# A 16-expert layer behind two transformer blocks on one core: where the modulation's matrix product runs

## The chip, the core and the metric

One Trainium2 chip, one of its cores. The metric is device time in microseconds, the median of the runs; lower is better. The engines are TensorE (matmuls, PE in the profile; PEld is its weight load), VectorE (DVE), ScalarE (ACT), GpSimd (POOL) and SyncE (SP), which here only issues transfers.

## The reference, cut to what matters

256 tokens of width 1024 pass through a first block (FFN, a token mixer with three attentions, FFN) and a second one (a mixer with a long convolution and a recurrence, then 16 experts of which each takes 32 tokens). Everything is float32. The second block is modulated by a vector c, and a context by c_ctx:

```python
def modulation(cvec, p):
    return jnp.split(jax.nn.silu(cvec) @ p['mod_w'] + p['mod_b'], 6, axis=-1)

m_lat = modulation(c[:, None, :], p)      # mod_w: 1024 x 6144
m_ctx = modulation(c_ctx, p)
h = rmsnorm(x, p['norm1_pre']) * (1.0 + m_lat[1]) + m_lat[0]
mixed, _ = token_mixer_2(h, p, ctx_states)
x = x + m_lat[2] * rmsnorm(mixed, p['norm1_post'])
h2 = rmsnorm(x, p['norm2_pre']) * (1.0 + m_lat[4]) + m_lat[3]
x = x + m_lat[5] * rmsnorm(expert_choice_moe(h2, p), p['norm2_post'])
```

So one or two rows are multiplied with a matrix of 1024 x 6144, 25 MB. The context needs parts 0 and 1 alone.

## The kernel before, in words

The stages follow each other: first FFN (to about 310 us), attention mixer (to about 640), second FFN (to about 880), second mixer (to about 1180), experts (to the end).

`ffn` (L365) walks over the hidden width in 11 groups of 256 columns. For each group four weight tiles of 128 x 1024 are loaded by SP (`wraw`, four buffers, rows of 1 KB), ScalarE copies each to a rounded high part `wh`, VectorE subtracts it for the low part `wl` (`wsplit`, L261; two buffers each), and TensorE makes three products per tile pair, hh with wh, hl with wh and hh with wl (`proj_feat_acc`, L292, its matmuls at L299, L301, L302): 96 matmuls a group. ScalarE and VectorE then form the gated product (L390 to L392), and at the end of group i `hooks.get(i)` is called: it traces other work there. Hook -1 is called before the first group. Behind the groups `wide` (L335) makes the down projection.

`modulation` (L797) is a generator. It treats mod_w in three blocks of 2048 columns: block 0 holds parts 0 and 1, block 1 parts 2 and 3, block 2 parts 4 and 5. It makes `sc`, 128 x 8 x 32, of which columns 0 and 1 are silu(c) and silu(c_ctx) and the rest zero. Per block the matrix comes in 16 pieces of 128 x 1024 (`mraw`, three buffers, 512 KB, rows of 4 KB), issued from GpSimd's queue at L835.

- Block 0 is traced in the first FFN's hook -1 (`start`, L1882). Each piece holds two column quarters of 512; TensorE multiplies each with `sc` into a column group of its own (32 columns of the array, 32 partitions of the PSUM tile `px`), L839. A matmul of float32 is two records in the trace.
- Blocks 1 and 2 are traced in the second FFN (`filter_and_modulation`, L1896, and hooks 6 and 10). Each piece is scaled by ScalarE (L842, L846) and added to `acc` by GpSimd (L847), or scaled and added by VectorE (L844, for k = 4). When all pieces are in, TensorE sums over the partitions with a column of ones, four quarters, L852.

At the end of a block the bias `m` is added, for blocks 1 and 2 the norm gains `nr` are worked in, and the rows go to DRAM (`mrows`, L867); the loads of `m` (L824) and `nr` (L861) and the stores are issued from ScalarE's queue. `psX`, the PSUM pool of `px`, has two banks; in the second FFN the convolution's filter (`hyena_filter`, L1304) uses it too: its sine layers ahead of the modulation, its second half behind it.

The order of each engine's instructions is set by a planner: it goes through its own estimate of the times and gives an engine, of the instructions that are ready by that estimate, the one that was traced first. On the chip each engine then takes its instructions in that order. Where work is traced, and so where a generator yields, is its rank.

Of the kernel before, what the change touches and what calls it, by code (L numbers as in the profile page):

```python
# [11 lines left out]
F32 = mybir.dt.float32  # L12
F32R = mybir.dt.float32r
I32 = mybir.dt.int32
ALU = mybir.AluOpType
AF = mybir.ActivationFunctionType
# [4 lines left out]
KC = 8  # L21
DFF = 2816
# [12 lines left out]
POOL_SHARE = 256  # L35
HOOK0 = 3
HOOK1 = 4
HOOK2 = 6
HOOK3 = 10
LGS = 4  # L40
GATHERS = {0: 1, 1: 1, 2: 2, 4: 2, 6: 2}
RINGS = (1, 2, 1, 2, 2, 4, 1, 3, 1, 1, 1)
# [123 lines left out]
def _body(nc, tc, ctx, A, out):  # L166
    V, S, G, PE = nc.vector, nc.scalar, nc.gpsimd, nc.tensor
# [10 lines left out]
    psX = ctx.enter_context(tc.tile_pool(name="psX", bufs=2, space=PSUM))  # L178
# [7 lines left out]
    xt = []  # L186
# [12 lines left out]
    def P(name, i=0, n=1):  # L199
        a = PP_COLS[name][0]  # L200
        return pp[:, a + i:a + i + n]
# [116 lines left out]
    def new_hT():  # L318
        return (hpool.tile([128, KC, T], F32R, name="hh"), hpool.tile([128, KC, T], F32R, name="hl"))
# [477 lines left out]
    def modulation(side, blocks, after=None):  # L797

        with ExitStack() as fx:
            tmp = fx.enter_context(tc.tile_pool(name="md_t", bufs=1, side=side))
            cr = tmp.tile([16, 128], F32, name="cr")
            S.dma_start(cr, A["c2"])
            th = tmp.tile([16, 128], F32, name="cth")
            S.activation(th, cr, AF.Tanh, scale=0.5)
            V.tensor_scalar(th, th, 0.5, 0.5, op0=ALU.mult, op1=ALU.add)
            V.tensor_tensor(cr, cr, th, op=ALU.mult)
            pt = psT.tile([128, 4, 128], F32, name="tr")  # L810
            PE.transpose(pt[:, 0, :16], cr, ident[:16, :16])
            sc = tmp.tile([128, KC, 32], F32, name="sc")
            V.memset(sc, 0.0)
            V.tensor_copy(sc[:, :, 0], pt[:, 0, 0:8])
            V.tensor_copy(sc[:, :, 1], pt[:, 0, 8:16])
            one = tmp.tile([128, 32], F32, name="one")
            V.memset(one, 0.0)
            V.memset(one[:, 0:1], 1.0)
            mbv = A["mod_b_2"].rearrange("(b g n) -> b g n", b=3, g=4)
            for b in blocks:  # L820
                m = tmp.tile([128, 512], F32, name="m")
                V.memset(m, 0.0)
                for g in range(4):
                    S.dma_start(m[32 * g:32 * g + 2, :], mbv[b, g:g + 1, :].to_broadcast([2, 512]))  # L824
                if b:
                    acc = tmp.tile([128, 2048], F32, name="acc")
                else:
                    ps = psX.tile([128, 512], F32, name="px")
                for k in range(KC):
                    for hf in range(2):  # L830
                        raw = tmp.tile([128, 1024], F32, name="mraw", bufs=3)
                        if after is not None and 2 * k + hf < 3:
                            G.tensor_copy(raw[:, 0:1], after)
                        hs = slice(hf * 1024, hf * 1024 + 1024)
                        G.dma_start(raw, A["mod_w_2"][k * 128:(k + 1) * 128, b * 2048 + hf * 1024:b * 2048 + hf * 1024 + 1024])  # L835
                        if b == 0:
                            for gg in range(2):
                                g = hf * 2 + gg
                                PE.matmul(ps[32 * g:32 * g + 32, :], sc[:, k, :], raw[:, gg * 512:gg * 512 + 512],  # L839
                                          start=(k == 0), stop=(k == KC - 1), skip_group_check=True)  # L840
                        elif k == 0:
                            S.activation(acc[:, hs], raw, AF.Copy, scale=sc[:, k, 0:1])  # L842
                        elif k % 4 == 0:
                            V.scalar_tensor_tensor(acc[:, hs], raw, sc[:, k, 0:1], acc[:, hs], op0=ALU.mult, op1=ALU.add)  # L844
                        else:
                            S.activation(raw, raw, AF.Copy, scale=sc[:, k, 0:1])  # L846
                            G.tensor_tensor(acc[:, hs], acc[:, hs], raw, op=ALU.add)  # L847
                if b:
                    yield
                    ps = psX.tile([128, 512], F32, name="px")  # L850
                    for g in range(4):
                        PE.matmul(ps[32 * g:32 * g + 32, :], one, acc[:, g * 512:g * 512 + 512], start=True, stop=True,  # L852
                                  skip_group_check=True)
                V.tensor_tensor(m, ps, m, op=ALU.add)
                if b:
                    nr = tmp.tile([128, 512], F32, name="nr")
                    V.memset(nr, 1.0)
                    for v in range(2):
                        nm = (None, ("norm1_post_2", None), ("norm2_pre_2", "norm2_post_2"))[b][v]
                        for g in range(2 * v, 2 * v + 2 if nm else 0):  # L860
                            S.dma_start(nr[32 * g:32 * g + 1, :], A[nm].rearrange("(h n) -> h n", h=2)[g % 2:g % 2 + 1, :])  # L861
                    lo, hi = m[0:64], m[64:128]
                    V.scalar_tensor_tensor(lo, lo, 0.5 if b == 1 else 1.0, nr[0:64], op0=ALU.mult if b == 1 else ALU.add,
                                           op1=ALU.mult)
                    V.tensor_tensor(hi, hi, nr[64:128], op=ALU.mult)
                for g in range(4):
                    S.dma_start(mrows[b * 4 + g:b * 4 + g + 1, :], m[32 * g:32 * g + 1, :])  # L867
                if b:
                    continue
                pt = psT.tile([128, 4, 128], F32, name="tr")  # L870
                for q in range(4):
                    PE.transpose(pt[:, q, :], m[:, q * 128:(q + 1) * 128], ident)
                mT = tmp.tile([128, 4, 4, 2], F32, name="mT")
                V.tensor_copy(mT, pt.rearrange("p q (g r) -> p q g r", g=4)[:, :, :, 0:2])

                n1 = P("n1pre", 0, 8).rearrange("p (g q) -> p g q", q=4)
                for r in range(2):
                    mv = mT.rearrange("p q g r -> p r g q")[:, r]
                    V.scalar_tensor_tensor(mfm[:, r, 0, :].rearrange("p (g q) -> p g q", q=4), mv[:, 2:4, :], 1.0,
                                           n1, op0=ALU.add, op1=ALU.mult)  # L880
                    V.tensor_copy(mfm[:, r, 1, :].rearrange("p (g q) -> p g q", q=4), mv[:, 0:2, :])
# [5 lines left out]
    def norm_mod_T(hT, t, x, r, xn, us, dense=True):  # L887

        rs = rsqrt(mean_sq_halves(x, xn), 128, 1, 1e-6)
        last = V.tensor_scalar(xn, x, rs, None, op0=ALU.mult)  # L890
        sl = slice(t * 128, (t + 1) * 128)

        def put(j0, k, ps):
            u = us(j0)
            for j in range(k):
                c = j0 + j
                if j0 and dense:
                    S.activation(u[:, j, :], ps[:, j, :], AF.Identity, scale=mfm[:, r, 0, c:c + 1],
                                 bias=mfm[:, r, 1, c:c + 1])
                else:  # L900
                    V.tensor_scalar(u[:, j, :], ps[:, j, :], mfm[:, r, 0, c:c + 1], mfm[:, r, 1, c:c + 1],
                                    op0=ALU.mult, op1=ALU.add)
            split(hT[0][:, j0:j0 + k, sl], hT[1][:, j0:j0 + k, sl], u)
        return last, lambda: transposes(put, xn, KC, dense)
# [975 lines left out]
    mods = []  # L1880
# [8 lines left out]
    hT2 = attention(xt, hT1, A["ffn2_norm"])  # L1889
# [15 lines left out]

    hT3 = []

    def norm_mod(pool, scratch):
        hT3.extend(new_hT())
        us = [scratch[:, 2 * D + i * 512:2 * D + i * 512 + 512].rearrange("p (a b) -> p a b", a=4) for i in range(4)]  # L1910

        normed = []

        def after(t):
            normed.append(norm_mod_T(hT3, t, xt[t], 0, scratch[:, t * D:(t + 1) * D], lambda j0: us[t * 2 + j0 // 4]))
            if t:
                in_turn(normed)
                next(filt[0], None)
        return after

    ffn(xt, hT2, None, A["ffn2_w_gate"], A["ffn2_w_up"], A["ffn2_w_down"], {-1: filter_and_modulation, HOOK2: lambda: next(mods[1]), HOOK3: lambda: next(mods[1], None)}, norm_mod)
    moe(xt, w1, *mixer2(xt, hT3, *spec, spx, w1, rowp[0]))
```

## Time and profile before

| | |
|---|---|
| median of 3 runs | 2133.89 us (2133.49 to 2136.44) |
| profiled execution, its own time | 2137.52 us |
| span of the profile | 2135.7 us |
| TensorE busy | 1710.0 us (80%) |
| VectorE busy | 867.6 us (41%) |
| ScalarE busy | 571.9 us (27%) |
| GpSimd busy | 291.4 us (14%) |
| moved by DMA | 600.71 MB, mean 281 GB/s |

The busy shares are means over stages with different limits; which engine is late in a stage has to be read from that stage. The profile is one execution; its time lies 3.6 us above the median, so what is worked out on it is moved by that much before it is compared.

### The profile page before, as it was taken

Reading aid. Unit: us, or ns where it says so; the run is one execution under the profiler, and the core shown is the slowest. Engines: PE = TensorE matmul, PEld = TensorE weight load, DVE = VectorE, ACT = ScalarE, POOL = GpSimd, SP = SyncE. Lnnn points to the kernel's source line nnn. Section 1 sums busy time; section 2 is a strip of 40 time slices with the busy share of each in tenths; the row PEclk is TensorE's granted clock in tenths of the full one; section 3 lists DMA queues with packets and bytes.
Section 4 is the critical chain, followed back from the end, with each engine's and each line's share of the span. In section 5 each row is a group of like instructions: output and inputs, shape, how many; then the busy total and the mean of one; then the engine's idle time right before and its main releaser. Section 6 shows DMA issues by size and latency. Waiting matters only on the chain.

```text
span 2135.7 us, 28907 instructions
## 1 busy us (share of the span) xinstructions
PE 1710.0 (80%) x11745; PEld 1024.6 (48%) x11746; DVE 867.6 (41%) x1593; ACT 571.9 (27%) x918; POOL 291.4 (14%) x280
## 2 busy tenths in 40 slices
PE   7999988999988899899889775666666666766664
PEld 5889867777768887788577410110111101111110
DVE  4668865975757675688846400000000000000001
ACT  3336443444436543454234200000000000000000
POOL 2111001210324650135213100000000000000000
PEclk9999999999989999999999888777767777667778
DMA  9664556444447864544447899999999999999997
GB/s 301 214 189 137 176 150 186 134 145 129 136 136 253 279 219 153 162 121 110 133 136 283 352 419 420 420 419 420 419 420 419 420 420 419 420 420 420 419 420 299
DMA packets 188695, 600.71 MB, mean 281 GB/s; under 512 B 36440, under 2 KB 92273, under 8 KB 139410
## 3 DMA queue, kind: packets, MB, share of 16 engines
q1 hardware_dynamic: 151312, 551.89, 68.4%
q0 software_dynamic: 10496, 36.08, 5.1%
q10 hardware_dynamic: 26754, 10.90, 1.9%
q8 instruction: 92, 1.51, 0.3%
q14 instruction: 41, 0.34, 0.0%
HBM read 593.25 MB, written 9.49 MB: 282 GB/s over the span
## 4 chain that ended last, share of the span: by engine, by line
DMA 44%; PE 38%; DVE 10%; ACT 3%; issue 3%; POOL 1%; ACTq 1%; SPq 0%; DVEq 0%; POOLq 0%
DMA ring<-exp_w 41%; PE mm L302 4%; PE mm L299 4%; PE mm L301 4%; PE mm L287 3%; PE mm L288 3%; PE mm L289 3%; DVE wl L246 3%; PE mm L346 2%; PE mm L349 2%; PE mm L345 2%; ACT wh L245 1%; PE px L1799 1%; PE mm L254 1%; PE px L839 1%
## 5 line engine op out<-in xcount | busy, mean ns | idle before, releaser
L1799 PE MATMUL px<-ring,xeT 128*32 128x512 f32 x2048 | 361.7, 797 | 185.6 <-DMA ring<-exp_w 185.5
L246 DVE TENSOR_TENSOR wl<-wraw,wh 128x1024 fp32r<-128x1024 f32 (+2 forms) x243 | 316.0, 1301 | 189.8 <-ACT wh L245 182.7
L245 ACT ACTIVATE wh<-wraw 128x1024 fp32r<-128x1024 f32 (+2 forms) x243 | 254.5, 1048 | 354.3 <-PE mm L301 152.3
L302 PE MATMUL mm<-hh,wl 128*128 128x256 f32 x912 | 266.8, 294 | 17.5 <-DVE wl L246 14.5
L1799 PEld LDWEIGHTS px<-ring,xeT 128*32 128x32 f32 x2048 | 49.5, 122 | 470.3 <-DMA ring<-exp_w 400.3
L299 PE MATMUL mm<-hh,wh 128*128 128x256 f32 x912 | 265.1, 291 | 6.0 <-ACT wh L245 3.9
L301 PE MATMUL mm<-hl,wh 128*128 128x256 f32 x912 | 264.0, 290 | 2.4 <-DVE hl L246 2.4
L1835 PE MATMUL tr<-ring,hid 128*32 128x512 f32 x1024 | 185.5, 828 | 96.4 <-DMA ring<-exp_w 83.8
L1811 DVE SCALAR_TENSOR_TENSOR mth<-mth,px 128x512 f32<-128x512 f32 x16 | 11.0, 688 | 553.9 <-ACT mth L1810 553.9
L302 PEld LDWEIGHTS mm<-hh,wl 128*128 128x128 f32 x912 | 178.6, 196 | 32.4 <-DVE wl L246 18.6
L299 PEld LDWEIGHTS mm<-hh,wh 128*128 128x128 f32 x912 | 179.4, 197 | 14.4 <-issue 7.1
L301 PEld LDWEIGHTS mm<-hl,wh 128*128 128x128 f32 x912 | 179.5, 197 | 7.3 <-issue 4.0
L1839 ACT ACTIVATE ye<-tr 128x512 f32<-128x512 f32 x16 | 9.6, 598 | 559.7 <-PE tr L1835 559.7
L1835 PEld LDWEIGHTS tr<-ring,hid 128*32 128x32 f32 x1024 | 26.6, 128 | 237.9 <-DMA ring<-exp_w 208.3
L288 PE MATMUL mm<-wl,hh 128*128 128x512 f32 (+2 forms) x320 | 128.5, 402 | 4.6 <-DVE wl L271 2.7
L287 PE MATMUL mm<-wh,hh 128*128 128x512 f32 (+2 forms) x320 | 119.7, 405 | 12.3 <-DVE rsq L226 6.5
L1645 POOL TENSOR_SCALAR rsz<-ss 128x1 f32<-128x1 f32 x2 | 0.6, 300 | 927.2 <-ACT ring L1645 927.1
L289 PE MATMUL mm<-wh,hl 128*128 128x512 f32 (+2 forms) x320 | 125.6, 394 | 0.0
L1812 DVE SCALAR_TENSOR_TENSOR mth<-mth,px 128x512 f32<-128x512 f32 x16 | 11.0, 687 | 254.4 <-PE px L1799 254.4
L1810 ACT ACTIVATE mth<-px 128x512 f32<-128x512 f32 x16 | 9.6, 597 | 279.6 <-PE px L1799 279.6
L287 PEld LDWEIGHTS mm<-wh,hh 128*128 128x128 f32 x320 | 59.8, 193 | 26.5 <-issue 9.8
L288 PEld LDWEIGHTS mm<-wl,hh 128*128 128x128 f32 x320 | 61.7, 193 | 20.2 <-DVE wl L271 4.1
(726 smaller groups left out, 2511.8 us busy)
## 6 DMA issues: line engine op xcount, KB each, us to landing
ring<-exp_w SPq DMA_DIRECT2D x384, 1024.0 KB
wraw<-w_in SPq DMA_DIRECT2D x107, 512.0 KB
mraw<-mod_w POOLq DMA_DIRECT2D x48, 512.0 KB, 5.1
wraw<-ffn_w_gate SPq DMA_DIRECT2D x44, 512.0 KB
wraw<-ffn_w_up SPq DMA_DIRECT2D x44, 512.0 KB
wraw<-ffn_w_down SPq DMA_DIRECT2D x44, 512.0 KB
wraw<-w_out SPq DMA_DIRECT2D x11, 512.0 KB
skew<-bd POOLq DMA_DIRECT2D x1, 3840.0 KB, 26.4
```

The source lines that it names most:

```text
L245: S.activation(dst_h, src, AF.Copy)
L246: (eng or V).tensor_tensor(dst_l, src, dst_h.bitcast(F32), op=ALU.subtract)
L287: PE.matmul(ps[t], hh[:, k, sl], wh, start=(k == 0), stop=False)
L288: PE.matmul(ps[t], hh[:, k, sl], wl, start=False, stop=False)
L289: PE.matmul(ps[t], hl[:, k, sl], wh, start=False, stop=(k == kc - 1))
L299: PE.matmul(o(c), wh[:, cs], hh[:, k, :], start=(k == 0 and bank0(c)), stop=False, skip_group_check=True)
L301: PE.matmul(o(c), wh[:, cs], hl[:, k, :], start=False, stop=False, skip_group_check=True)
L302: PE.matmul(o(c), wl[:, cs], hh[:, k, :], start=False, stop=(k == KC - 1), skip_group_check=True)
L345: PE.matmul(acc[t][nh], fh[:, sl], wh[:, ns], start=(k == 0), stop=False)
L346: PE.matmul(acc[t][nh], fh[:, sl], wl[:, ns], start=False, stop=False)
L1799: PE.matmul(ps[32 * g:32 * g + 32, :], xeT[:, k, es], wt[:, 0, g * 512:(g + 1) * 512], start=(k == 0), stop=(k == KC - 1), skip_group_chec ...
L1835: PE.matmul(pe2[32 * c:32 * c + 32, :], hid[:, 2 * h + j, 32 * g:32 * g + 32], w2t[:, j * 2 + nh, :], start=(g == 0 and h == 0), stop=(g = ...
```

## The change

All three blocks go through TensorE. A piece is now 128 x 2048 (8 KB rows, 1 MB, two buffers, 8 pieces a block), and its four quarters are multiplied with `sc` one behind the other, each in its column group. `acc`, `one` and the work of ScalarE, GpSimd and VectorE on the pieces go, and so do the four summing matmuls. For blocks 1 and 2 the generator yields after every piece: the first is traced in hook -1 of the second FFN, and every hook behind a group traces two more, so the 16 pieces are spent at hook 7. Block 0 stays in the first FFN's hook -1.

```diff
             for b in blocks:
...
-                if b:
-                    acc = tmp.tile([128, 2048], F32, name="acc")
-                else:
-                    ps = psX.tile([128, 512], F32, name="px")
+                ps = psX.tile([128, 512], F32, name="px")
                 for k in range(KC):
-                    for hf in range(2):
-                        raw = tmp.tile([128, 1024], F32, name="mraw", bufs=3)
-                        if after is not None and 2 * k + hf < 3:
-                            G.tensor_copy(raw[:, 0:1], after)
-                        hs = slice(hf * 1024, hf * 1024 + 1024)
-                        G.dma_start(raw, A["mod_w_2"][k * 128:(k + 1) * 128, b * 2048 + hf * 1024:b * 2048 + hf * 1024 + 1024])
-                        if b == 0:
-                            for gg in range(2):
-                                g = hf * 2 + gg
-                                PE.matmul(ps[32 * g:32 * g + 32, :], sc[:, k, :], raw[:, gg * 512:gg * 512 + 512],
-                                          start=(k == 0), stop=(k == KC - 1), skip_group_check=True)
-                        elif k == 0:
-                            S.activation(acc[:, hs], raw, AF.Copy, scale=sc[:, k, 0:1])
-                        elif k % 4 == 0:
-                            V.scalar_tensor_tensor(acc[:, hs], raw, sc[:, k, 0:1], acc[:, hs], op0=ALU.mult, op1=ALU.add)
-                        else:
-                            S.activation(raw, raw, AF.Copy, scale=sc[:, k, 0:1])
-                            G.tensor_tensor(acc[:, hs], acc[:, hs], raw, op=ALU.add)
-                if b:
-                    yield
-                    ps = psX.tile([128, 512], F32, name="px")
+                    raw = tmp.tile([128, 2048], F32, name="mraw", bufs=2)
+                    if after is not None and k < 2:
+                        G.tensor_copy(raw[:, 0:1], after)
+                    G.dma_start(raw, A["mod_w_2"][k * 128:(k + 1) * 128, b * 2048:b * 2048 + 2048])
                     for g in range(4):
-                        PE.matmul(ps[32 * g:32 * g + 32, :], one, acc[:, g * 512:g * 512 + 512], start=True, stop=True,
-                                  skip_group_check=True)
+                        PE.matmul(ps[32 * g:32 * g + 32, :], sc[:, k, :], raw[:, g * 512:g * 512 + 512],
+                                  start=(k == 0), stop=(k == KC - 1), skip_group_check=True)
+                    if b:
+                        yield
...
+    def two_more():
+        for _ in range(2):
+            next(mods[1], None)
...
-    ffn(xt, hT2, None, A["ffn2_w_gate"], A["ffn2_w_up"], A["ffn2_w_down"], {-1: filter_and_modulation, HOOK2: lambda: next(mods[1]), HOOK3: lambda: next(mods[1], None)}, norm_mod)
+    ffn(xt, hT2, None, A["ffn2_w_gate"], A["ffn2_w_up"], A["ffn2_w_down"], {-1: filter_and_modulation, **{i: two_more for i in range(DFF // 256)}}, norm_mod)
```

## Rows read from the trace of the kernel before

**Rows 1.** The page, 40 equal slices of the span: tenths of DMA engines' busy share.
```profile
DMA  9664556444447864544447899999999999999997
```
**Rows 2.** The page, chain that ended last: shares of the span by line.
```profile
DMA ring<-exp_w 41%; PE mm L302 4%; PE mm L299 4%; PE mm L301 4%; PE mm L287 3%; PE mm L288 3%; PE mm L289 3%; DVE wl L246 3%; PE mm L346 2%; PE mm L349 2%; PE mm L345 2%; ACT wh L245 1%; PE px L1799 1%; PE mm L254 1%; PE px L839 1%
```
**Rows 3.** Busy time by stretch: PE, PEld, DVE, ACT, POOL; PEclk, DMA share, GB/s.
```profile
17.00:76.00 59.00, 59.00 (x390) 43.45 (x390) 23.04 (x27) 16.54 (x20) 7.92 (x15) 1.00 0.83 268
...
1400.00:2100.00 700.00, 460.66 (x2400) 75.53 (x2396) 27.73 (x56) 18.95 (x36) 0.00 (x0) 0.73 1.01 420
```
**Rows 4.** Timeline of TensorE in the first FFN: start us, us, engine, line.
```profile
21.64 0.28 PE L302 MATMUL mm<-hh,wl 128*128 128x256 f32 x1
21.85 1.05 PE L839 MATMUL px<-mraw,sc 128*32 128x512 f32 x4
22.83 0.38 PE L299 MATMUL mm<-hh,wh 128*128 128x256 f32 x1
23.05 0.28 PE L301 MATMUL mm<-hl,wh 128*128 128x256 f32 x1
23.17 0.28 PE L302 MATMUL mm<-hh,wl 128*128 128x256 f32 x1
```
**Rows 5.** Timeline of TensorE in the experts' first products.
```profile
1216.13 3.64 PE L1799 MATMUL px<-ring,xeT 128*32 128x512 f32 x32
```
**Rows 6.** Tile mraw: durations ns min/median/max; who waited (us, times); its transfers.
```profile
L846 ACT ACTIVATE mraw<-mraw,sc x24: 1132/1137/1154, 656.3 to 774.3; 128x1024 f32<-128x1024 f32 x24
L847 POOL TENSOR_TENSOR acc<-acc,mraw x24: 2355/2408/3373, 657.5 to 775.6; 128x1024 f32<-128x1024 f32 x24
...
  POOL mraw L835: 71.9, 28
...
DMA to landing us min/median/max: 4.0/5.1/11.3
```
**Rows 7.** Busy time by stretch in the second FFN, columns as in rows 3.
```profile
660.00:673.00 13.00, 8.46 (x56) 8.05 (x55) 10.76 (x12) 7.95 (x10) 9.27 (x6) 0.87 0.71 218
673.00:727.00 54.00, 51.87 (x414) 49.11 (x414) 37.63 (x31) 32.51 (x33) 30.81 (x23) 1.00 0.86 279
727.00:745.00 18.00, 11.34 (x77) 10.64 (x76) 10.52 (x7) 7.85 (x9) 12.73 (x10) 0.81 0.73 232
745.00:777.00 32.00, 30.77 (x247) 29.18 (x245) 23.12 (x18) 20.36 (x21) 19.51 (x13) 1.00 0.89 295
```
**Rows 8.** Groups by line, 17 to 76 us, then 660 to 777: busy, mean ns.
```profile
L246 DVE TENSOR_TENSOR wl<-wraw,wh 128x1024 fp32r<-128x1024 f32 x13 | 15.9, 1226 | 27.9 <-ACT wh L245 25.2 <-PE px L839 2.8
...
L246 DVE TENSOR_TENSOR wl<-wraw,wh 128x1024 fp32r<-128x1024 f32 x34 | 58.1, 1714 | 26.1 <-ACT wh L245 26.0
```
**Rows 9.** Timeline of VectorE, and last one row of GpSimd's.
```profile
657.64 2.49 DVE L1328 TENSOR_SCALAR kf<-hid 64x256 f32<-64x256 f32 x1
660.16 0.29 DVE L1329 TENSOR_SCALAR kf<-kf 64x256 f32<-64x256 f32 x1
...
680.75 2.58 DVE L246 TENSOR_TENSOR wl<-wraw,wh 128x1024 fp32r<-128x1024 f32 x1 [1.30 <-ACT wh L245]
...
687.80 1.21 DVE L246 TENSOR_TENSOR wl<-wraw,wh 128x1024 fp32r<-128x1024 f32 x1
...
679.86 5.74 POOL L847 TENSOR_TENSOR acc<-acc,mraw 128x1024 f32<-128x1024 f32 x2 [5.69 <-ACT mraw L846]
```
**Rows 10.** Timelines of ScalarE and TensorE between blocks 1 and 2; idle before in brackets.
```profile
730.91 4.87 ACTq L824 DMA_DIRECT2D m<-mod_b  x4
736.15 1.15 ACT L846 ACTIVATE mraw<-mraw,sc 128x1024 f32<-128x1024 f32 x1 [4.57 <-DMA m<-mod_b]
...
738.30 0.58 PE L299 MATMUL mm<-hh,wh 128*128 128x256 f32 x1 [3.87 <-ACT wh L245]
...
740.88 0.58 PE L302 MATMUL mm<-hh,wl 128*128 128x256 f32 x1 [1.78 <-DVE wl L246]
```
**Rows 11.** Timeline of TensorE: one reducing step of the second FFN.
```profile
716.37 1.05 PE L852 MATMUL px<-acc,one 128*32 128x512 f32 x4
```

More of the change, by code (lines that the diff above doesn't have):

```diff
@@ L37 @@
 HOOK1 = 4
-HOOK2 = 6
-HOOK3 = 10
 LGS = 4
@@ L815, in modulation @@
             V.tensor_copy(sc[:, :, 1], pt[:, 0, 8:16])
-            one = tmp.tile([128, 32], F32, name="one")
-            V.memset(one, 0.0)
-            V.memset(one[:, 0:1], 1.0)
             mbv = A["mod_b_2"].rearrange("(b g n) -> b g n", b=3, g=4)
```

## The prediction

> **What bounds the kernel now.** I read the page's slices first, then the chain of waits, then the busy time by stretches, then single instructions. The slices show the DMA engines full from about slice 23 to the end [rows 1], and the chain gives 41% of the span to the experts' weight ring [rows 2]. In that tail 420 GB/s arrive and TensorE is only two thirds busy [rows 3]: the tail has a fixed length, and its start is what earlier stages can move. Ahead of it TensorE has the most to do. The change works in two places there, the gate/up part of the first FFN and that of the second.
>
> In the first FFN, 17 to 76 us, TensorE is busy for 59.00 of 59.00 us [rows 3]; in this stretch block 0 of the modulation already runs on TensorE. What one of its steps costs is seen in single matmuls [rows 4]. Ordinary matmuls start every 0.12 us (23.05 to 23.17). A modulation step (two column quarters, four matmul records) starts at 21.85 behind the matmul of 21.64, and the two matmuls behind it start at 22.83 and 23.05. Without the step the second of these would have started two intervals after 21.64, at 21.88: the step displaces what follows by 1.17 us. In the experts' matmuls four column quarters go at once, and 32 records, that is four steps of eight, take 3.64 us or 0.91 each [rows 5]. So four quarters cost TensorE no more than two do.
>
> In the second FFN blocks 1 and 2 run on ScalarE, GpSimd and VectorE instead: 24 scalings of 1.14 us and 24 additions of 2.41 us, beside a few that open a sum [rows 6]. While they run, TensorE loses time. The stretch 660 to 777 us, cut in four, holds 56, 414, 77 and 247 matmul records [rows 7]. At 0.12 us each, with 2.34 us for the two reducing steps in the second piece and 1.0 us for the one begun in the last, the loss is 13 - 6.7 = 6.3; 54 - 48.7 - 2.3 = 2.9; 18 - 9.2 = 8.8; 32 - 29.2 - 1.0 = 1.8: together 19.8 us.
>
> What makes them: the weight splits on VectorE, the subtraction that gives wl, take 1.23 us on average in the first FFN's stretch and 1.71 here [rows 8]. One of 680.75 took 2.58 us while a pair of GpSimd additions ran from 679.86, and one at 687.80, beside no addition, took 1.21; a small tensor_scalar of the filter's sine at 657.64 took 2.49 us, and one of the same shape at 660.16 took 0.29 [rows 9]. With two split buffers, some 5.8 us of matmuls, that delay reaches TensorE. The granted clock then drops to 0.87 and 0.81 of full speed in the first and third pieces [rows 7], so the matmuls behind a stall are slow as well. The third piece is of another kind: at the seam between blocks 1 and 2 ScalarE's queue issues the loads of the bias rows, 4.87 us from 730.91, and the next split waits behind them; TensorE sits for 3.87 and 1.78 us [rows 10].
>
> **The change, part by part, on the profiled execution's own 2137.52 us** (2135.7 us of span; 3.6 us above the median shown).
>
> *First FFN, block 0.* 16 steps of two quarters become 8 of four. By rows 4 and 5 a lone step of four costs what one of two does, 1.17 us. TensorE is the bound there, so 8 x 1.17 = 9.4 us go. Bounds: 0 if something else is late right behind it, 10.4 if the steps stand in pairs (16 x 1.17 - 4 x (1.17 + 0.91)). I take 9.4: nothing else is near, the splits of that stretch have 1.23 of every 2.9 us on VectorE. The loads are 8 of 1 MB in 2 buffers against 16 of 512 KB in 3, 2 MB in flight against 1.5. The context's chain begins after block 0 and moves with it.
>
> *Second FFN, added.* 16 steps of four quarters, 18.7 us if each stands alone, 8 x (1.17 + 0.91) = 16.6 us if the two of a hook stand together. I take 18.7. Here a rule speaks against the change. Rows 4 show 1.17 us for a step between ordinary matmuls, rows 5 show 0.91 for one inside a stream of its own kind. The Trainium skill, TensorEngine Tiling (Array Packing), Key Properties, says that changing the tiling mode drains TensorE; the trace agrees with 0.26 us a step. With no drain the addition would be 16 x 0.91 = 14.6 us, with it 18.7.
>
> *Second FFN, removed from TensorE.* Four reducing steps like the one at 716.37 [rows 11] (two a block): 4 x 1.17 = 4.7 us.
>
> *Second FFN, removed elsewhere.* ScalarE gives up the scalings, GpSimd the additions. None of these is on the path itself; what counts is the stalls they cause. In the first piece the sine's steps lose their inflated lengths (about 2.2 us for the one at 657.64, the same order for two others): I take 5 of 6.3, and leave the rest to the table loads of ScalarE. In the second and last piece VectorE's splits are back at 1.2 us: 4 of 4.7. In the seam the queue of ScalarE still issues the same small loads, and only the scaling of 1.15 us at 736.15 [rows 10] and the slow subtraction behind it go: 4.4 of 8.8. Sum 13.4 us. Bounds: 4 (only the second kind goes) and 19.8 (all).
>
> *New waits.* A step on TensorE now stands in order behind a load of 1 MB, and what is queued behind it is the next group's matmuls. In block 0 before, TensorE never sat idle for these loads: the loads waited for their buffers' users (71.9 us over the three blocks [rows 6]), and in block 0 that was TensorE, as the planner puts a step later than the 5.1 us in which 512 KB landed. 1 MB lands in at most double that, 10.2 us, against a group of 96 x 0.12 = 11.5 us plus two steps of 1.17, 13.9 us, in which two loads have to come. I take nothing, with the price under the rivals. One PSUM bank of two is held through a block; the filter's second half, the only other user, waited for the second block before as well. The small DMAs of ScalarE stay. DMA bytes stay; the DMA engines' share was 0.71 to 0.89 in the four pieces [rows 7], and the first FFN ran at 0.83 with no stall [rows 3].
>
> Sum: -9.4 + 18.7 - 4.7 - 13.4 = -8.8 us. 2137.5 - 8.8 = 2128.7 on its own time, and 3.6 less on the median's scale: 2125 us. The tail is of fixed length, so the gain arrives whole at the end.
>
> **The rivals.**
> *A, all stalls go and the steps pair up.* For it: with the scalings away the seam has slack, and the first FFN's stretch, built the same way, has no stall. Against it: the seam's loads are unchanged. -10.4 + 16.6 - 4.7 - 19.8 = -18.3 us, 2116.
> *B, slower: TensorE waits in order for the 1 MB loads.* Place: each hook of the second FFN. A buffer comes free only when its step ran, two loads are in flight beside 2 MB of weights per group, and the engines' share of 0.89 leaves little. It decides from the point where a load's round trip exceeds the 13.9 us of a group and its steps; then eight hooks stall, at about 2.5 us (the middle between the seam's 1.78 and 3.87), and each is followed by matmuls at half clock: the third piece's 0.81 of 18 us is 6.8 us at half speed for its stalls together, up to 3.4 us lost, so some 1.5 us a stall. 8 x 4 = 32 us. The sum is then -8.8 + 32 = +23: 2157. Against it: block 0 of before, where the waits were the other way round. What a 1 MB load of GpSimd's queue takes is shown by no row. The Trainium skill, DMA: Bandwidth & Descriptors, Anatomy of one DMA, fits a GpSimd-issued load as 2.0 us plus its bytes at 436 GB/s. As an estimate from that page, 512 KB would take 3.2 us and 1 MB 4.4; the trace's 5.1 for 512 KB is above it, beside other traffic. By the page the load grows by 1.2 us and B does not come; by doubling it grows by 5.1 and B is near.
> *C, the stalls stay.* If ScalarE's and VectorE's own order (sine, table loads, seam) makes them and not the additions, only 4 us go: -9.4 + 18.7 - 4.7 - 4 = +0.6, 2134, no change. Against it: rows 9.
> *D, the first FFN's gain does not carry*, as the context's chain or the attention's start is late then: +0.6, also 2134. Against it: the stages behind are TensorE's too.
>
> **How the numbers follow.** Forecast 0.45, A 0.23, B 0.14, C 0.12, D 0.06. About 0.2%, 4.3 us, is what can be told from no change here: below 2129.6 is faster, above 2138.2 slower. Forecast and A are faster, 0.68; C and D the same, 0.18; B slower, 0.14. The range takes in A and the top of C and D with some us on each side, 2113 to 2138, and leaves B out; the forecast's own range is 2120 to 2130.
>
> **What would show it.** Right: steps of eight records 0.98 to 1.1 us long in both FFNs; wl subtractions near 1.2 us throughout the second; no idle time of TensorE put down to them; the first FFN's gate/up shorter by about 9 us, the second's within a few us of now; the ring's first caught-up expert earlier by the sum. Wrong: idle time of TensorE before the steps, released by the modulation's loads (B); subtractions of 2.5 us with GpSimd quiet (C); a first FFN that ends at the same time, or an attention that takes up the gain (D); a seam without idle time (A).

## The result and the profile after

The changed kernel takes 2119.01 us (median of 4 runs, 2116.38 to 2122.53) against 2135.03 (2133.49 to 2136.44, 4 runs on the same chip): a ratio of 0.9927, with a 95% interval of 0.9914 to 0.994. The profiled execution took 2120.70 us, with a span of 2118.9: 16.8 us less than the profiled one of before. The forecast was 2125, with -8.8 us on the profiles' own time. Faster was right; the forecast gain is little more than half of the measured one (-8.8 beside -16.0 of the medians).

The page of the kernel after, its DMA slices and its chain, answer to [rows 1, 2]: the ring of experts' weights holds the tail as before, and the line of the steps (L826, L839 before) has 1% of the chain as before.

```profile
DMA  9845636544459666433358899999999999999997
...
DMA ring<-exp_w 42%; PE mm L300 4%; PE mm L297 4%; PE mm L299 4%; PE mm L285 3%; PE mm L286 3%; PE mm L287 3%; PE mm L344 2%; PE mm L343 2%; PE mm L347 2%; DVE wl L244 1%; DVE wl L269 1%; PE px L826 1%; PE mm L252 1%; ACT wh L243 1%
```

Where the time went is read from busy time by stage. The stages are cut at the first matmul of each: gate/up of the first FFN; its down projection and the attention; gate/up of the second FFN; its down projection and norm; the second mixer; the experts. Columns as in [rows 3]. First the kernel before:

```profile
14.30:237.60 223.30, 213.02 (x1874) 189.31 (x1874) 145.35 (x232) 95.00 (x150) 30.66 (x40) 0.98 0.64 199
237.60:634.80 397.20, 370.54 (x2391) 291.57 (x2389) 272.98 (x671) 181.25 (x311) 57.35 (x50) 0.97 0.49 148
634.80:796.20 161.40, 146.19 (x1083) 135.32 (x1083) 111.96 (x109) 89.89 (x96) 88.26 (x67) 0.95 0.78 250
796.20:879.10 82.90, 76.78 (x314) 56.72 (x313) 50.52 (x63) 36.27 (x52) 6.92 (x7) 0.97 0.52 168
879.10:1195.90 316.80, 278.64 (x2716) 234.71 (x2717) 228.32 (x399) 128.90 (x229) 96.97 (x94) 0.94 0.53 167
1195.90:2135.70 939.80, 620.86 (x3360) 113.67 (x3360) 51.69 (x104) 32.73 (x65) 6.00 (x9) 0.75 0.99 411
```

The same stages of the kernel after:

```profile
13.80:222.30 208.50, 201.21 (x1873) 185.19 (x1873) 144.92 (x233) 95.02 (x150) 25.75 (x33) 1.00 0.68 214
222.30:616.40 394.10, 367.86 (x2391) 290.21 (x2389) 272.37 (x672) 180.97 (x311) 59.57 (x50) 0.97 0.50 150
616.40:781.90 165.50, 165.35 (x1223) 137.72 (x1223) 89.71 (x109) 58.49 (x66) 20.44 (x29) 0.99 0.76 246
781.90:852.10 70.20, 63.98 (x286) 51.87 (x284) 43.67 (x56) 36.30 (x52) 2.57 (x4) 0.97 0.60 195
852.10:1177.90 325.80, 285.47 (x2716) 240.24 (x2717) 228.45 (x399) 128.92 (x229) 98.12 (x94) 0.91 0.51 163
1177.90:2118.90 941.00, 617.10 (x3360) 113.10 (x3360) 51.68 (x104) 32.72 (x65) 6.03 (x9) 0.75 0.99 410
```

Gate/up of the second FFN: TensorE was busy 146.19 of 161.40 us and now 165.35 of 165.50. It has 140 records more (1223 for 1083) and almost no idle time. Its down part is 12.7 us shorter, with 28 records fewer. These are one fact: the filter's second half, which stood beside the down projection, now runs in gate/up. Records of its kind cost much the same in either place, four in 1.88 us before and eight in 3.60 after, some 0.45 each. The second half has 28 of them, 12.6 us, moved and not saved.

```profile
811.73 1.88 PE L1373 MATMUL px<-fm,dft 128*128 128x512 f32 x4
```
```profile
706.21 3.60 PE L1342 MATMUL px<-ab,one 128*128 128x512 f32 x8
```

So the second FFN as a whole is what counts: 244.3 to 235.7 us, -8.6. The balance of the profiles is then: start -0.5, first gate/up -14.8, attention -3.1, second FFN -8.6, mixer +9.0, tail +1.2, together -16.8. How much of each is the change's and how much that of one execution, the repeats below tell.

One step of the kernel after (timeline of TensorE, answering to [rows 4]), and its splits and steps in gate/up of the second FFN (groups by line, answering to [rows 8]):

```profile
714.91 0.28 PE L299 MATMUL mm<-hl,wh 128*128 128x256 f32 x1
715.03 0.28 PE L300 MATMUL mm<-hh,wl 128*128 128x256 f32 x1
715.24 1.07 PE L826 MATMUL px<-mraw,sc 128*32 128x512 f32 x8
716.24 0.38 PE L297 MATMUL mm<-hh,wh 128*128 128x256 f32 x1
716.46 0.28 PE L299 MATMUL mm<-hl,wh 128*128 128x256 f32 x1
```
```profile
L244 DVE TENSOR_TENSOR wl<-wraw,wh 128x1024 fp32r<-128x1024 f32 x43 | 52.6, 1224 | 49.9 <-ACT wh L243 49.7 <-PE mm L300 0.2
...
L826 PE MATMUL px<-mraw,sc 128*32 128x512 f32 x128 | 17.0, 605 | 0.0
```

The step of four quarters displaces 716.46 - (715.03 + 0.24) = 1.19 us, where two quarters displaced 1.17 before: twice the columns at the same price. All 24 steps of the kernel after stand alone like this one, none right behind another. The splits take 1.22 us where [rows 8] had 1.71; over the whole gate/up the kernel before had 1.63:

```profile
L246 DVE TENSOR_TENSOR wl<-wraw,wh 128x1024 fp32r<-128x1024 f32 x43 | 69.9, 1629 | 32.7 <-ACT wh L245 32.6
```

The loads of the kernel after, in the view of tile mraw (what the issuing engine waited for; then who waited for the tile):

```profile
  PE px L826: 84.7, 17
  PE mm L300: 30.8, 3
...
  POOL mraw L824: 84.7, 17
...
DMA to landing us min/median/max: 5.1/7.2/10.2
```

The loads wait for their buffers' users, 84.7 us in 17 waits; TensorE is not among those who waited for a load. 1 MB lands in 7.2 us (median), where 512 KB took 5.1 [rows 6], and never over 10.2.

### The profile page after: what moved, and what is told of

It reads as the page before. It is cut to its first block, busy times and chain, and to the rows that moved or that the text cites. A ratio compares the mean times of both kernels' runs of the same rounds, so it can differ in the third digit from the quotient of the medians.

```text
span 2118.9 us, 28998 instructions
## 1 busy us (share of the span) xinstructions
PE 1704.9 (80%) x11857; PEld 1021.7 (48%) x11858; DVE 837.5 (40%) x1585; ACT 540.5 (26%) x888; POOL 217.2 (10%) x231
## 4 chain that ended last, share of the span: by engine, by line
DMA 45%; PE 36%; DVE 8%; issue 3%; ACT 2%; POOL 1%; ACTq 1%; DVEq 0%; SPq 0%; POOLq 0%
DMA ring<-exp_w 42%; PE mm L300 4%; PE mm L297 4%; PE mm L299 4%; PE mm L285 3%; PE mm L286 3%; PE mm L287 3%; PE mm L344 2%; PE mm L343 2%; PE mm L347 2%; DVE wl L244 1%; DVE wl L269 1%; PE px L826 1%; PE mm L252 1%; ACT wh L243 1%
## 5 line engine op out<-in xcount | busy, mean ns | idle before, releaser
L244 DVE TENSOR_TENSOR wl<-wraw,wh 128x1024 fp32r<-128x1024 f32 (+2 forms) x243 | 297.7, 1225 | 193.0 <-ACT wh L243 191.6
L297 PEld LDWEIGHTS mm<-hh,wh 128*128 128x128 f32 x912 | 179.0, 196 | 16.8 <-issue 12.8
```

The costliest lines, as they stand in the source:

```text
L244: (eng or V).tensor_tensor(dst_l, src, dst_h.bitcast(F32), op=ALU.subtract)
L297: PE.matmul(o(c), wh[:, cs], hh[:, k, :], start=(k == 0 and bank0(c)), stop=False, skip_group_check=True)
```

## The experiments

**Each half alone.** One kernel with only block 0 new, one with only blocks 1 and 2 new.

```diff
 e1:                 for k in range(KC):
+                    if b == 0:
+                        raw = tmp.tile([128, 2048], F32, name="mraw", bufs=2)
...
+                        continue
                     for hf in range(2):
```


> Only block 0 is changed (8 steps of four quarters from 1 MB loads); blocks 1 and 2 are as before. Theory 1, the two halves of the change are separate gains: the first FFN's gate/up falls from 222.9 us to about 208, as in the changed kernel (9.4 of steps, some 5 of stalls behind them), the second FFN stays at 244, and the whole gains 10 to 15 us. Rival, the first FFN's further 5 us are chance of the planner's order: the gate/up falls to 213 only, the whole by 9. Rival D of the prediction (it does not carry): gate/up 213 or less, the whole unchanged.

```diff
 e2:                for k in range(KC):
+                    if b == 0:
+                        for hf in range(2):
+                            raw = tmp.tile([128, 1024], F32, name="mraw", bufs=3)
...
+                        continue
                     raw = tmp.tile([128, 2048], F32, name="mraw", bufs=2)
...
```


> Block 0 as before (16 steps of two quarters, 512 KB loads), blocks 1 and 2 as in the changed kernel. Theory 1: the first FFN's gate/up stays at 223, the second FFN (its first matmul to the second mixer's first) falls from 244.3 to about 236, the whole gains 3 to 9 us. If the second mixer's 9 us that the changed kernel loses belong to the second half of the change, the mixer is at 326 here and the whole does not move; if they belong to the planner's order alone, the mixer may stand anywhere between 316 and 326.

Block 0 alone: 2121.46 us, ratio 0.9933 (0.9917 to 0.995). Blocks 1 and 2 alone: 2133.06, ratio 0.9986 (0.9976 to 0.9997). Against the 2135.49 of before on the same chip that is -14.0 and -2.4: the two add up to the whole's -16.0, and most of it comes with block 0. In the first the first gate/up took 208.8 us, as in after; in the second 220.7, as in before. The attention behind it does not take up block 0's gain (395.0 us in the first, 394.1 in after, 397.2 and 395.7 in the two profiles of before): rival D falls. With blocks 1 and 2 alone the second FFN took 238.0 us, 6 to 8 less than before. By stage the parts do not add up: block 0 alone changed the second FFN too (237.4, with its code untouched, and its splits still at 1.67 us), as the planner placed its work otherwise.

**What makes the stalls.** Before, without GpSimd's 24 additions (the sums of blocks 1 and 2 are incomplete), and before, without ScalarE's 24 scalings (the additions add unscaled rows).

```diff
 e3:
-                            G.tensor_tensor(acc[:, hs], acc[:, hs], raw, op=ALU.add)
 e4:
-                            S.activation(raw, raw, AF.Copy, scale=sc[:, k, 0:1])
```


> The kernel before without GpSimd's 24 additions in blocks 1 and 2 (the sums of those blocks are incomplete; ScalarE's scalings, the loads and the reducing steps stay). Theory 1, the additions slow VectorE and so stall TensorE: wl subtractions in the second FFN back from 1.71 to about 1.23 us, the stalls at the sine and in the middle go (some 10 of the 19.8 us), the seam stays; the second FFN falls by 8 to 12. Rival C, ScalarE's and VectorE's own order makes the stalls: less than 4 us change.

> The kernel before without ScalarE's 24 scalings (the pieces are added unscaled; GpSimd's additions, loads and reducing steps stay). Theory 1: wl subtractions stay slow where an addition runs beside them (mean over 1.6 us), so the stalls at the sine and in the middle stay; the seam's stall of 3.87 us shrinks, the second FFN falls by 0 to 6. Rival, ScalarE's load makes the stalls: the second FFN falls by 10 or more with the subtractions still slow.

Without the additions: 2122.72, ratio 0.9944 (0.9928 to 0.9961). Without the scalings: 2140.88, 1.0026 (1.0014 to 1.0038), with a second FFN of 249.1 us, longer by 3 to 5 where 0 to 6 less had been expected. The splits of the second gate/up, first without additions, then without scalings:

```profile
L246 DVE TENSOR_TENSOR wl<-wraw,wh 128x1024 fp32r<-128x1024 f32 x43 | 53.3, 1240 | 44.5 <-ACT wh L245 44.3
```
```profile
L246 DVE TENSOR_TENSOR wl<-wraw,wh 128x1024 fp32r<-128x1024 f32 x43 | 80.1, 1862 | 31.9 <-ACT wh L245 31.6
```

GpSimd's additions slow VectorE's splits; ScalarE's scalings do not, and C, which held VectorE's and ScalarE's own order to be the cause, falls. The single splits of before say the same: the 24 that overlap an addition take 1.92 us on average, the 19 others 1.26. Without the additions the second FFN took 226.7 us, 17.6 less than in the first profile of before, more than the 8 to 12 expected; TensorE's idle time in gate/up fell from 15.2 to 1.9 us. The 17.6 us are what the additions cost together with what the planner's new order brought, which is not shown apart: block 0 alone moved this stage by 7 us.

**The rows.** After, with each piece of 1 MB in two transfers of 4 KB rows; and, since that had changed more than the rows, with one transfer of 4 KB rows (of blocks b and b + 3 in halves, so that other columns reach the sums).

```diff
 e5:
-                    G.dma_start(raw, A["mod_w_2"][k * 128:(k + 1) * 128, b * 2048:b * 2048 + 2048])
+                    for hf in range(2):
+                        hs = slice(hf * 1024, hf * 1024 + 1024)
+                        G.dma_start(raw[:, hs], A["mod_w_2"][k * 128:(k + 1) * 128, b * 2048 + hf * 1024:b * 2048 + hf * 1024 + 1024])
 e9:
-                    G.dma_start(raw, A["mod_w_2"][k * 128:(k + 1) * 128, b * 2048:b * 2048 + 2048])
+                    G.dma_start(raw.rearrange("p (a n) -> p a n", n=1024),
+                                A["mod_w_2"][k * 128:(k + 1) * 128].rearrange("p (a n) -> p a n", n=1024)[:, b:b + 4:3, :])
```


> The changed kernel with each piece of 1 MB fetched in two transfers of 4 KB rows. Theory: TensorE never waits for the pieces in the changed kernel (the loads wait for TensorE, 84.7 us in all), so the row length is worth nothing: first FFN's gate/up within 3 us of 208.5, second FFN within 3 us of 235.7, the whole within 4 us of the changed kernel. Rival: the DMA engines, 0.9 of the time busy in the first FFN's start, need the longer rows; then both FFNs are longer by 3 us or more, with idle time of TensorE put down to weight loads or pieces.

> After, with each piece of 1 MB still one transfer, but from rows of 4 KB in place of 8 KB: a piece holds the 128 rows of blocks b and b+3 in halves, so the columns that reach the sums are others (the bytes are as many, each read once; the modulation's values are not the reference's). The order of TensorE's work is that of after. Theory (TensorE bounds both FFN stages, loads are hidden): same as after, 2119 within 4 us, TensorE's steps unchanged, a load perhaps longer than the 7.2 us median of after. Rival (the 8 KB rows are a cause of the gain, as 16 engines move 8 KB pieces better): 2125 or more, with TensorE idle before steps for the loads.

The first took 2144.63 us, ratio 1.0043 (1.0028 to 1.0058). It is no test of the rows: with two transfers the planner put each step's two halves apart, and TensorE's records of the second gate/up were busy 28.5 us and not 17.0; half of the first load also escaped the one-column copy that holds it back (it was issued at 1.3 us, not 9.8), and the first FFN started at 21.6 us, not 13.9. It priced instead the step of two quarters: the second FFN was 13.4 us longer than in after. Its line of the steps:

```profile
L828 PE MATMUL px<-mraw,sc 128*32 128x512 f32 x128 | 28.5, 605 | 0.0
```

The second, with TensorE's order as in after, took 2122.11 us, ratio 0.9935 (0.992 to 0.9951). Its loads, and who waited:

```profile
  POOL mraw L824: 83.0, 17
  DVE m L831: 2.6, 3
  PEld px L827: 1.1, 1
  PE px L827: 0.9, 1
...
DMA to landing us min/median/max: 5.4/7.9/10.7
```

A load takes 0.7 us longer, and TensorE waits for it once, 1.1 us. The interval holds after's ratio: that the rows are 8 KB long does not make the gain.

**The spreading.** After, with all pieces of blocks 1 and 2 issued ahead of the first group, where after issues two per group.

```diff
 e6:
-        next(mods[1])
+        for _ in mods[1]:
+            pass
```


> The changed kernel with all 16 pieces of blocks 1 and 2 traced ahead of the second FFN's groups, nothing spread. Theory: the planner sets a step where its own estimate has the piece landed, so the steps come in the pace of the loads, some 5 us each, and end near 80 us instead of 110 us into the FFN; TensorE is full either way, so the second FFN is at 236 within 4 us. Rival: the spreading is needed; pieces and weights then share the DMA engines at their limit, TensorE waits, and the second FFN is over 242.

2120.01 us, ratio 0.9923 (0.9908 to 0.9937): as after. The hooks are worth nothing here; the planner spreads the steps by itself, from 635 to 720 us where after has them from 634 to 725. That they would end some 80 us into the stage was wrong: it is over 100.

**Does TensorE bound the second FFN?** After, with the 16 steps of blocks 1 and 2 made twice (the sums are doubled).

```diff
 e7:
-                                  start=(k == 0), stop=(k == KC - 1), skip_group_check=True)
+                                  start=(k == 0), stop=(k == KC - 1 and not b), skip_group_check=True)
+                    for g in range(4 if b else 0):
+                        PE.matmul(ps[32 * g:32 * g + 32, :], sc[:, k, :], raw[:, g * 512:g * 512 + 512],
+                                  start=False, stop=(k == KC - 1), skip_group_check=True)
```


> The changed kernel with each step of blocks 1 and 2 made twice in a row (their sums are doubled). It prices a step by itself: 16 further ones of 0.91 us behind their like, 14.6 us, if TensorE is the bound of the whole second FFN: 235.7 to 250, the whole longer by 14 to 15. Rival: TensorE has slack there and the steps were paid from it; then less than 8 us.

2143.14 us, ratio 1.0039 (1.0026 to 1.0051) to before. Gate/up and down part, by stretch:

```profile
619.70:800.70 181.00, 180.85 (x1352) 141.42 (x1352) 89.79 (x109) 58.72 (x66) 20.47 (x29) 0.99 0.68 225
800.70:871.40 70.70, 63.97 (x286) 51.91 (x284) 43.61 (x55) 36.16 (x52) 2.57 (x4) 0.96 0.61 194
```

16 more steps make gate/up 15.5 us longer, 0.97 each: right behind another step, so between the 0.91 of [rows 5] and the lone 1.19. TensorE stays busy throughout, 180.85 of 181.00 us, and in this stage every step is paid in full. The whole, though, is 24.1 us longer than after, not the 14 to 15 expected: the second FFN gives 16.0, and the mixer, 330.5 us in this profile with its code untouched, 4.7 to 11.1 more (by the two profiles of after).

**The mixer, whose code nobody touched.** Before with HOOK2 = 8 in place of 6: the same work, ordered otherwise. And both kernels once more, unchanged, for a second profile.

```diff
 e8:
-HOOK2 = 6
+HOOK2 = 8
```


> The kernel before with the reducing step of block 1 traced at hook 8 instead of 6: the same work, but the planner's order of the second mixer changes with it. Theory: the second mixer's length (316.8 us before, 319 to 326 in all others) follows the planner's order: here it is over 319 too, with the second FFN within 5 us of 244. Rival: the mixer's loss comes with the steps on TensorE or the earlier filter; then it stays within 2 us of 316.8.

> The kernel before once more, unchanged, for a second profile of its stages. Theory (one profile's stages vary by some 3 us with no change of work or order): the first FFN's gate/up comes to 220 to 221 us against the 223.3 of the first profile, as in the four other kernels that have the same first FFN, and the second mixer, 316.8 in the first profile, to between 316 and 320. Rival (the stages of the first profile are the kernel's own): 223 and 317 within 1 us, so that the change is worth 14.8 us in the first FFN and costs 9 in the mixer.

> The changed kernel once more, unchanged. Theory: the first FFN's gate/up 208 to 209 us and the second FFN's stage 235 to 237 as in the first profile, since nothing in them waits; the second mixer between 321.9 (the kernel with the modulation's work not spread, whose TensorE order in the mixer is the same) and 325.8 (the first profile). Rival: a mixer near 317, so that its 9 us were the execution's alone and no cost of the changed order. Time 2119 within 3 us, ratio to before 0.991 to 0.994.

HOOK2 = 8: 2148.20 us, ratio 1.0054 (1.0039 to 1.0069). The mixer took 327.6 us where it had 316.8 (318.1 in the second profile of before). Part is one wait, by the waits of TensorE in that stage; first the kernel before, then HOOK2 = 8 (us in total, times, longest):

```profile
PE mm L287 <- DVE gg L1521: 3.9, 1, 3.9
```
```profile
PE mm L287 <- DVE gg L1521: 8.6, 1, 8.6
```

The repeats: before 2135.0 us (one run), after 2120.58, ratio 0.9929 (0.9912 to 0.9946). The second profile of before:

```profile
14.00:233.70 219.70, 210.77 (x1873) 187.03 (x1873) 145.19 (x232) 95.33 (x150) 29.72 (x40) 1.00 0.65 203
233.70:629.40 395.70, 369.40 (x2390) 291.10 (x2388) 273.22 (x671) 181.44 (x311) 57.41 (x50) 0.97 0.49 149
629.40:792.50 163.10, 147.30 (x1083) 136.41 (x1083) 112.00 (x109) 90.06 (x96) 88.31 (x67) 0.94 0.77 248
792.50:875.40 82.90, 77.39 (x314) 57.48 (x312) 50.52 (x63) 36.18 (x52) 6.93 (x7) 0.96 0.53 168
875.40:1193.50 318.10, 281.38 (x2715) 237.13 (x2717) 228.21 (x399) 129.07 (x229) 97.24 (x93) 0.93 0.52 167
1193.50:2133.20 939.70, 619.13 (x3360) 112.17 (x3360) 51.93 (x104) 32.73 (x65) 6.04 (x9) 0.75 0.99 410
```

And of after:

```profile
13.80:222.50 208.70, 201.63 (x1873) 186.38 (x1873) 144.72 (x232) 94.85 (x150) 26.27 (x33) 0.99 0.67 214
222.50:617.70 395.20, 369.04 (x2390) 291.04 (x2388) 273.31 (x672) 181.00 (x311) 58.47 (x50) 0.97 0.50 149
617.70:783.40 165.70, 165.56 (x1224) 137.90 (x1224) 89.88 (x109) 58.59 (x66) 20.41 (x29) 0.99 0.75 245
783.40:853.40 70.00, 63.69 (x286) 51.64 (x284) 43.70 (x56) 36.20 (x52) 2.57 (x4) 0.97 0.60 196
853.40:1172.80 319.40, 278.46 (x2715) 235.39 (x2716) 227.92 (x399) 128.85 (x229) 97.63 (x93) 0.94 0.52 166
1172.80:2113.60 940.80, 619.13 (x3360) 112.47 (x3360) 51.74 (x104) 32.69 (x65) 6.02 (x9) 0.75 0.99 410
```

Both FFN stages of after repeat within 0.2 us. The first gate/up of before does not: 223.3, then 219.7 (and 219.7 to 220.7 in the four experiments that have it unchanged). The mixer of after does not either: 325.8 at a granted clock of 0.91, then 319.4 at 0.94, the same program. TensorE's idle time there is much the same in both (40.3 and 40.9 us), its busy time is not (285.47 and 278.46): the difference lies in matmuls that took longer while less of the clock was granted, and what lowered the clock is not shown. The expectation had 321.9 as its lower end and missed. By the second pair the balance is: start -0.2, first gate/up -11.0, attention -0.5, second FFN -10.3, mixer +1.3, tail +1.1, together -19.6 of 2133.2.

## Why the prediction was right, and where its size was off

*First gate/up, -9.4.* Right in mechanism, and below what was measured: -14.8 by the first pair, -11.0 by the second, whose 219.7 us of before is the usual one. Counted from matmul start to matmul start, the steps themselves fell from 15.7 to 8.0 us and the FFN's own matmuls from 142.8 to 140.7 in the second pair, -9.8 together, beside 9.4 worked out. Some 3 us more come from the context's matmuls (31.5 to 28.3 us in that count), which wait less in the new order; the forecast had them only move along. The stage's other matmuls take some 2 us more. A step of four costs what one of two did, 1.19 beside 1.17.

*Second FFN, added: 18.7.* All 16 steps stand alone, so the lone price holds: 16 x 1.19 = 19.0. The forecast's term stands.

*Second FFN, stalls removed: -13.4.* This is the term that was mis-sized. All of the 19.8 us counted went, and some more. Gate/up with the filter's 12.6 us taken out is 152.9 us against 161.4, or -8.5; with the steps at 19.0 and the reducing steps at -4.7, the stalls must have given 8.5 + 19.0 - 4.7 = 22.8. The idle time of TensorE alone fell by 15.1 us (15.2 to 0.15). Of the other 7.7 some 6 are matmuls at the lower clock, an estimate from the granted clock of the stage, 0.95 of 146.19 busy us before and 0.99 of 165.35 after. That all stalls go is rival A's term; its sum for the second FFN, 16.6 - 4.7 - 19.8 = -7.9, is the nearest of all to -8.6 and -10.3.

The step that failed was the seam, "the queue of ScalarE still issues the same small loads", with 4.4 us left to them. The issue of the four bias rows is still there, and takes 1.15 us, not 4.87. The row of after:

```profile
688.95 1.15 ACTq L818 DMA_DIRECT2D m<-mod_b  x4
```

The trace of before held the answer: its own first issue of the same four, for block 1, had taken no longer, and I had looked only at the seam. What stretched the second is in the chain of before, in order of time:

```profile
636.73 1.18 ACTq L824 DMA_DIRECT2D m<-mod_b  x4
```
```profile
728.63 6.88 DMA wraw<-ffn_w_up
```

So 4.87 was no price but a wait. Three of the four issues had gone out by 731.84; the fourth waited for a semaphore on which that load of weights reports its landing, too. The load landed at 728.63 + 6.88 = 735.51, and the fourth issue began at 735.54, with the next scaling and the next copy to `wh` behind it in ScalarE's order. The second profile of before (5.72 us) and HOOK2 = 8 (3.8) show the same: the fourth issue begins 0.02 to 0.03 us after the landing of such a load. In after, in e1, e3 and e4 the four take 1.1 to 1.2 us. So the wait goes with the order of the work, and the forecast had carried it over as a fixed cost. The filter's sine lost its stalls, too: TensorE is idle for 0.15 us in all of gate/up.

*Fixed tail.* 939.8 us before, 941.0 and 940.8 after: right, within some 1 us.

*B, TensorE waits for the 1 MB loads.* It did not come: 7.2 us at the median and 10.2 at most, under the 13.9 of a group. Doubling 5.1 gave the upper end, and the largest lies just there. The fit of the Trainium skill (DMA: Bandwidth & Descriptors, Anatomy of one DMA) makes an estimate of 4.4 us for 1 MB; under the other traffic of this kernel the trace has 7.2, 2.1 more than for 512 KB, where the fit has 1.2 more.

*Why the total still fell inside the range.* The second pair of profiles gives -19.6, close to A's -18.3, and the medians -16.0 and -15.0. The forecast's own range, 2120 to 2130, is missed by 1 us; the wide one held because it took in A. Two errors also met, and that is luck. The two FFN stages of the forecast gained more than its -8.8: -23.4 us by the first pair, -21.3 by the second, which from 2133.9 would have led to 2110.5 or 2112.6, under the range. And the mixer, which was to pass the gain on whole, gave back 9.0 or 1.3 us. How much of that is the new order and how much the granted clock of one execution is not settled: six profiles with after's order of TensorE there, but for a few records (after, its repeat, e1, e5, e6, e9), spread from 319.3 to 325.8 by themselves, and the two of before stand at 316.8 and 318.1.

## What to carry to other kernels

In this kernel, where TensorE already streams weights at its bound, a step of four column groups displaced hardly more than one of two (1.19 beside 1.17 us): fill the groups before adding steps. Before work is left on GpSimd because it "has time", look at what VectorE's instructions cost beside it: the stalls that went were worth some 22.8 us to the second FFN. Count, too, what the move puts on the bound engine: the 16 steps took 19.0 of them back, and with the 4.7 of the reducing steps some 8.5 remained. And when one row is to price an operation that stays, look up the other executions of the same line first, and whether its length is work or a wait; compare stages over two profiles of each kernel before a stage that was not touched is given a cause.

## What the runs showed that was not expected

The planner's order moves untouched stages: HOOK2 alone lengthened the second mixer by 9.5 to 10.8 us with no change of work, and block 0 alone shortened the second FFN by 7 to 9. The same program's mixer differed by 6.4 us between two executions, at granted clocks of 0.91 and 0.94. In before GpSimd's additions lengthened a split of 1.22 us to 1.63 on average, and without the scalings (e4) to 1.86: there the same 24 additions overlap the splits for 40.1 us, in before for 24.8.
